# The down product in three stages with some k pairs by seven products

## The chip, the cores and the metric

The kernel runs on one core of a Trainium2 chip. The metric is the device time of one execution in microseconds. TensorE (PE) multiplies, VectorE (DVE) and ScalarE (ACT) work element by element, and the queue of SyncE (SP) starts the loads. Weights stream from the chip's main memory (HBM) into on-chip memory (SBUF); products are accumulated in eight banks (PSUM).

## The reference

One layer of a decoder on 256 tokens of width 2048, in float32. After a recurrent mixer and an attention mixer have been added to the residual stream, a feed-forward network follows, which is what the change touches:

```python
h = rmsnorm(x, g_ffn[i])
gu = h @ w_ffn_gu[i]                 # 2048 -> 2 x 5632
g, u = jnp.split(gu, 2, axis=-1)
x = x + (jax.nn.silu(g) * u) @ w_ffn_down[i]   # 5632 -> 2048
ple_gate = jax.nn.sigmoid(rmsnorm(x, g_ple[i]) @ w_ple_gate[i])
x = x + ple_gate * (p[i] @ w_ple_proj[i])
```

## The kernel before

Everything is cut into tiles of 128. The 256 tokens are two token tiles, the inner dimension of a product is a row of k tiles (44 for the down product), and the output columns are handled 1024 at a time: a *group* is two blocks of 512 columns for both token tiles, so four output blocks, each in one PSUM bank (called "2", "4", "3", "8" in the code).

**A product in three matmuls.** Each float32 operand is split into a high part that PE takes exactly and a low remainder. One 128 x 128 x 512 product is then three matmuls, high by high, high by low and low by high (`prod`, lines 565 to 567). The tokens are the stationary operand, 512 columns of weights move.

**Two ways to do k tiles.** A *plain* k tile gives four products (two token tiles, two column blocks). A *pair* of k tiles can also be done as a 2 x 2 block product by seven products in place of eight (the method of Strassen and Winograd). Its slots carry names: "11", "21" and "22" for plain quadrants of the weights, "T1" to "T4" for sums of quadrants. The weight sums are made on DVE (`summed`, lines 251 to 281), the sums on the token side by `half_sums` (line 569) once per pair. A list of slots says in which order a group works through its sums and plain k tiles; a number in it is a plain k tile. `SEVEN` (line 33) does the pairs 0 and 1 of 16 k tiles by seven products. `SEVEN3` (line 34) does three pairs, where ("S", i, p) are slots of the single pair p. "11", "T2" and "T3" are accumulated in a fifth bank "B", one on top of the other: after each, ACT copies the bank's state into a tile (`group`, line 632), and the differences of these states are later added to or subtracted from the output blocks. In `wo` this adding is done by `fold`, straight into the residual tiles `x1`.

**The stream of weights.** `PLAN` lists every weight tile in the order of use, cut into chunks of up to 1024 columns (one slot of a group is one chunk). `Stream.need` issues loads eight chunks ahead and splits four chunks ahead: ACT makes the high part `whi` (line 296), DVE the low part `wlo` (line 297), each in four buffers. A buffer comes free when PE is done with its chunk. Plain chunks are loaded into the pool `p32`; the quadrants of sum slots go into the pool of tag Q (26 tiles of 1024 columns), which also holds the normed input `hg`, its sums `hsum` and the activations `acts`. The tag H (21 tiles of 512) holds `x1` and the copies of banks.

**The order.** Instructions are emitted in program order; a planner that knows estimated durations sets the order on each engine before the launch and may move independent instructions past each other. `pend` is a list of small pieces of work (transposes of what the last group made) of which each group takes one per slot from its fourth slot on.

**The feed-forward part** is the last third of `TAIL` (lines 172 and 173): eleven gate and up groups of 512 hidden columns each (`gu`, line 1113, three pairs by seven products over 16 k tiles), each giving two pairs of activation k tiles, and between them the down product, which adds to `x1` what the finished activations give. Before, it comes in four stages of 12, 12, 12 and 8 k tiles, two groups each, and all its k tiles are plain (`down`, line 1133): behind gu 3, gu 6, gu 10 and the third stage. The stage dn0 does not need the activations of gu 3, which precedes it. After the last stage, `next_h` (line 1071) turns `x1` into `h3`, the input of the last product, pg.

Of the kernel before, what the change touches and what calls it, by code (L numbers as in the profile page):

```python
# [11 lines left out]
ALU = mybir.AluOpType  # L12

P = 128
S = 256
# [11 lines left out]
NPR = KR // 2  # L27
NPD = KD // 2
NHP = 8
FQ = [12, 12, 12, 8]  # L30
FQ0 = [0, 12, 24, 36]
NG = 11
SEVEN = ["11", "T1", "21", 4, 5, "22", 6, 7, "T2", 8, 9, "T3", 10, 11, "T4", 12, 13, 14, 15]
SEVEN3 = ["11", ("S", 1, 2), "T1", "21", ("S", 2, 2), 6, "T2", 7, "22", 8, ("S", 3, 2), 9, "T3", 10,
          ("S", 4, 2), 11, "T4", 12, 13, 14, 15]
LONG = ["11", "T1", "21", 4, 5, "22", 6, 7, 8, "T2", 9, 10, 11, "T3", 12, 13, 14, "T4", 15, 16, 17, 18, 19, 20, 21]
TWO = (0, 1)
LAST_GROUP = ("pg", 1)
# [3 lines left out]

def pairs_of(name):

    return (0, 1, 2) if name == "gu" else (0, 1)


# [2 lines left out]
    return isinstance(x, str) or isinstance(x, tuple) and x[0] == "S"  # L50


def products(x):


    if isinstance(x, int):
        return [("2", (x, 0), None, 0), ("4", (x, 1), None, 0), ("3", (x, 0), None, 1), ("8", (x, 1), None, 1)]
    bank = {"11": "B", "T1": "8", "T2": "B", "T3": "B", "21": "2", "22": "3", "T4": "4"}
    if isinstance(x, str):
        return [(bank[x], x, p, c) for c, p in enumerate(TWO)]  # L60
    k = {1: ("11", "21"), 2: ("T1", "T2"), 3: ("22", "T3"), 4: ("T4",)}[x[1]]
    return [(bank[y], y, x[2], c) for c, y in enumerate(k)]

# [22 lines left out]
def plan():  # L86

    out = []

    def dense(w, m, ks, tag=0, nt=2):  # L90
        out.append(((w, m, tag), [(w, k, m + e) for k in ks for e in range(nt)]))

    def proj(c0, p):
        dense("in", c0 + 2 * p, range(KD))

    def gates(p):
        t = []
        for w in ("rga", "rgx"):
            for e in range(2):
                t += [(w, k, 2 * p + e) for k in rg_k_tiles(2 * p + e)]  # L100
        if len(t) <= 16:
            out.append((("rg", p), t))
        else:
            h = len(t) // 2
            out.append((("rg", p), t[:h]))
            out.append((("rg2", p), t[h:]))

    def block(c0, b):

        out.append((("blk", c0, b), [("in", k, c0 + 4 * b + e) for k in range(KD) for e in range(4)]))  # L110

    def tokens(name, g, w, cols, slots):


        for x in slots:
            if isinstance(x, int):
                t = [(w, x, m) for c in cols for m in c]
            elif x[0] == "x":
                t = [("pp", k, m) for k in range(2) for m in cols[x[1]]]
            elif isinstance(x, tuple):  # L120
                p = 2 * x[2]
                t = {1: [(p, 0), (p + 1, 0)], 2: [(p + 1, 1), (p, 1)]}.get(x[1], [])
                t = [(w, k, m) for k, c in t for m in cols[c]]
            elif x in ("T2", "T3", "T4"):
                t = []
            else:
                r, c = {"11": (0, 0), "21": (1, 0), "22": (1, 1), "T1": (0, 1)}[x]
                t = [(w, 2 * p + r, m) for p in TWO for m in cols[c]]
            out.append((("tok", name, g, x), t))

    for stage, g, w, c0, c1, slots in HEAD:
        tokens(stage, g, w, [list(range(c, c + 4)) for c in (c0, c1)], slots)
    proj(C_XR, 0)
    proj(C_XR, 1)
    for p in range(NPR):
        proj(C_GR, p)
        if p + 2 < NPR:
            proj(C_XR, p + 2)
        gates(p)
        if p in GATE_R_AT:  # L140
            block(C_GTR, GATE_R_AT[p])

    for stage, g, w, c0, c1, slots in TAIL:
        if w is None:
            block(c0, g)
            continue
        tokens(stage, g, w, [list(range(c, c + 4)) for c in (c0, c1)], slots)
    return out
# [4 lines left out]
def tail():  # L153


    def wide(name, w, slots, c=0):
        return [(name, g, w, c + 8 * g, c + 8 * g + 4, slots[g]) for g in range(2)]

    def blocks(*cs):
        return [("blk", b, None, c, None, None) for c, b in cs]  # L160

    def gu(*gs):
        return [("gu", g, "gu", 4 * g, 44 + 4 * g, SEVEN3) for g in gs]

    def dn(q):
        return wide(f"dn{q}", "dn", [list(range(FQ0[q], FQ0[q] + FQ[q]))] * 2)

    x = [("x", 0), ("x", 1)]
    plain = [list(range(KD))] * 2
    return (wide("ro", "ro", [LONG] * 2) + wide("v", "in", [SEVEN] * 2, C_V)  # L170
            + blocks(*[(c, b) for b in range(4) for c in (C_Q, C_K)], *[(C_GTA, b) for b in range(4)])
            + wide("ao", "ao", plain) + wide("wo", "wo", [SEVEN] * 2) + gu(0, 1, 2, 3) + dn(0) + gu(4, 5, 6) + dn(1)
            + gu(7, 8, 9, 10) + dn(2) + dn(3)
            + wide("pg", "pg", [SEVEN[:-3] + x + SEVEN[-3:]] * 2))


# [166 lines left out]
def tile_hybrid_block(ctx: ExitStack, tc: tile.TileContext, xT: bass.AP, x: bass.AP, pT: bass.AP,  # L343
# [25 lines left out]
    def tt(o, a, b, op):  # L369
        nc.vector.tensor_tensor(o, a, b, op)  # L370
# [48 lines left out]
    for n in ("h", "l"):  # L419
        t = cst.tile([P, 512], F32R, tag=f"w1{n}", name=f"w1{n}")  # L420
# [25 lines left out]
    def parts(t):  # L446
        v = t.rearrange("p (e x s) -> p e x s", e=2, x=2)
        return v[:, :, 0, :], v[:, :, 1, :]
# [4 lines left out]
    def split(src, tag):  # L453
        t = tl(tag, F32R)
        hi, lo = parts(t)
        actv(hi, pair(src), AF.Copy)
        tt(lo, pair(src), f32(hi), ALU.subtract)
        return t
# [152 lines left out]
    xg = []  # L611
# [20 lines left out]
    def group(at, pairs, sums, after=None, also=()):  # L632
# [6 lines left out]
        name, g = at  # L639
        slots = [x for n, y, _, _, _, sl in HEAD + TAIL if (n, y) == at for x in sl  # L640
                 if isinstance(x, int) or is_sum(x)]
        seq = [(n, q) for n, x in enumerate(slots) for q in products(x)]
        if at == LAST_GROUP:
            k = len(slots) - 3
            rest = [q for q in seq if q[0] >= k]
# [210 lines left out]
        tt(c22, q8, c22, ALU.subtract)  # L856
        return c11, c21, c12, c22

    def xg_sums(p):
        h = tl("T")  # L860
        hi, lo = parts(xg[p])
        tt(pair(h), f32(hi), f32(lo), ALU.add)
        xsum[p] = half_sums(h)

    def last_gate():
        with behind_splits():
# [5 lines left out]

    n = len(LONG)
    for g in range(2):
        also = {n - 2 + i: (lambda p: lambda: xg_sums(p))(p) for i, p in enumerate(pairs_of("v"))} if g else {
            8: last_gate, 12: next_table}
        for i, c in enumerate(whole(("ro", g), y, ysum, also)):
            o = gtr[2 * g + i // 2][i % 2]
            tt(o, c, o, ALU.mult)
# [168 lines left out]
    x1 = [[None] * 4 for _ in range(2)]  # L1048
    ssq = [cst.tile([P, 8], F32, tag=f"ssq{i}", name=f"ssq{i}") for i in range(2)]

    def squares(i, t, b):
        q = tl("T")
        actv(q, x1[t][b], AF.Square, accum_out=ssq[i][:, 2 * b + t:2 * b + t + 1])
# [36 lines left out]
    for g in range(2):  # L1090
        for b in (2 * g, 2 * g + 1):
            for t in range(2):
                x1[t][b] = tl("C")
                nc.sync.dma_start(x1[t][b], x[t * P:t * P + P, b * 512:b * 512 + 512])

        def fold(tiles):
            for n, (c, op) in enumerate((("11", ALU.add), ("T3", ALU.add), ("T1", ALU.add),
                                         ("T3", ALU.subtract))):
                o = x1[n % 2][2 * g + n // 2]
                tt(o, o, tiles[c], op)  # L1100

        for n, ps in enumerate(group(("wo", g), mix, msum, fold)[0]):
            t, b = n % 2, 2 * g + n // 2
            tt(x1[t][b], ps, x1[t][b], ALU.add)
            squares(0, t, b)
        for p in range(4 * g, 4 * g + 4):
            pend.append(next_h(hg, hsum, p, PC_GF))
    token_scales(0, rs1)


    acts = {}

    def gu(g):
        c11, c21, c12, c22 = whole(("gu", g), hg, hsum)
        for c, t in ((c11, 0), (c21, 1)):
            actv(c, c, AF.Silu, scale=rs1[:, t:t + 1])
        for c, t, s_ in ((c12, 0, c11), (c22, 1, c21)):
            stt(c, c, rs1[:, t:t + 1], s_, ALU.mult, ALU.mult)

        def turn(f):  # L1120
            def run():
                ps = psum()
                for e in range(2):
                    for t, a in enumerate((c12, c22)):
                        c = (2 * f + e) * P
                        o = e * 256 + t * P
                        nc.tensor.transpose(ps[:, o:o + P], a[:, c:c + P], ident)  # L1127
                acts[2 * g + f] = split(ps, "A" if (2 * g + f) % 11 < 8 else "B")
            return run

        pend.extend(turn(f) for f in range(2))

    def down(q, g):
        for n, ps in enumerate(group((f"dn{q}", g), acts, None)[0]):
            t, b = n % 2, 2 * g + n // 2
            tt(x1[t][b], ps, x1[t][b], ALU.add)
            if q == 3:
                squares(1, t, b)
        if q == 3:
            for p in range(4 * g, 4 * g + 4):  # L1140
                pend.append(next_h(h3, sum3, p, PC_GP))

# [105 lines left out]
```

## Time and profile before

| | |
|---|---|
| median of 3 runs | 1884.11 us (1883.82 to 1884.48) |
| profiled execution, own time | 1884.7 us |
| its span | 1883.0 us |
| mean granted clock of TensorE | 0.998 |
| busy PE, DVE, ACT | 1873.4, 1377.9, 1158.5 us |
| matmuls | 9000 |
| main memory read | 357.69 MB |

A row of the view of groups reads: line, engine, operation, result <- operands (by the program's tile names), partitions x elements, xcount | busy time of the group in us, mean ns of one | idle time of the engine ahead of it and what ended it. Since matmuls are pipelined, the time from start to end of one is longer than its share of PE. In the view by stretches a row is one stretch of time (from:to in us from the span's start), its length, and for each engine its busy time and its count of instructions. A row of the timeline is start, length, engine, line, operation. Most token and weight work goes through helpers, so that line 370 is every `tensor_tensor` of the tiles and line 376 every activation of the main part.

### The profile page before, as it was taken

The page shows a single profiled execution, that of the slowest core. Times are in us where ns is not written, and L with a number is a line of the kernel's source. Part 1 is how long each engine was busy: PE and PEld are TensorE (multiplying, and loading weights), DVE is VectorE, ACT ScalarE, POOL GpSimd, SP SyncE. Part 2 cuts the span into 40 slices and gives each one's busy share as a digit, 9 for nine tenths or more (in the row PEclk, how much of TensorE's full clock was granted, in tenths as well). Part 3 has the DMA queues.
Part 4 walks back from the last instruction along what each step waited for, and adds up shares of the span by engine and source line. Part 5 has one row for each costly group of instructions (what it writes and reads, how often), then busy time and mean ns, then how long its engine had stood idle before and what let it go on. Part 6 is the DMA issues. An engine that isn't in the chain of part 4 may idle for free.

```text
span 1883.0 us, 24009 instructions
## 1 busy us (share of the span) xinstructions
PE 1873.4 (99%) x9000; PEld 1576.0 (84%) x9000; DVE 1377.9 (73%) x1649; ACT 1158.5 (62%) x1535; POOL 2.2 (0%) x9
## 2 busy tenths in 40 slices
PE   9999999999999999999999999999999999999998
PEld 7899989888888888888888888888888888888886
DVE  7688887677776576665578988767886688855776
ACT  6688888764554566776356765644554466543673
POOL 0000000000000000000000000000000000000000
PEclk9999999999999999999999999999999999999999
DMA  7456555665545545445556565375447645465554
GB/s 275 180 181 197 191 178 192 231 210 196 205 156 191 190 158 167 157 157 179 190 216 227 189 239 211 129 262 210 173 145 263 211 151 216 148 214 193 168 192 140
DMA packets 101925, 361.36 MB, mean 192 GB/s; under 512 B 11440, under 2 KB 12080, under 8 KB 101808
## 3 DMA queue, kind: packets, MB, share of 16 engines
q1 hardware_dynamic: 101664, 359.82, 55.4%
q8 instruction: 70, 1.15, 0.2%
q14 instruction: 47, 0.39, 0.1%
q10 hardware_dynamic: 144, 0.01, 0.0%
HBM read 357.69 MB, written 2.10 MB: 191 GB/s over the span
## 4 chain that ended last, share of the span: by engine, by line
PE 99%; DMA 0%; DVE 0%; SPq 0%; ACT 0%; issue 0%; DVEq 0%
PE ps L567 27%; PE ps L566 27%; PE ps L565 27%; PE ps L495 9%; PE ps L499 4%; PE ps L479 1%; PE ps L478 1%; PE ps L477 1%; PE ps L1127 1%; DMA w<-in_w_dram 0%; PE ps L919 0%; PE ps L1068 0%; DVE H L370 0%; PE ps L1030 0%; PE ps L973 0%; PE ps L972 0%
## 5 line engine op out<-in xcount | busy, mean ns | idle before, releaser
L297 DVE TENSOR_TENSOR wlo<-w,whi 128x1024 fp32r<-128x1024 f32 (+1 forms) x580 | 701.1, 1215 | 370.1 <-ACT whi L296 365.2
L296 ACT ACTIVATE whi<-w 128x1024 fp32r<-128x1024 f32 (+1 forms) x580 | 607.4, 1052 | 461.9 <-PE ps L567 402.4
L566 PE MATMUL ps<-wlo,Q 128*128 128x512 f32 x2223 | 866.4, 390 | 0.1
L567 PE MATMUL ps<-whi,Q 128*128 128x512 f32 x2223 | 866.0, 390 | 0.0
L565 PE MATMUL ps<-whi,Q 128*128 128x512 f32 x2223 | 792.5, 392 | 0.0
L566 PEld LDWEIGHTS ps<-wlo,Q 128*128 128x128 f32 x2223 | 417.5, 188 | 86.4 <-DVE wlo L297 1.3
L567 PEld LDWEIGHTS ps<-whi,Q 128*128 128x128 f32 x2223 | 417.4, 188 | 86.6
L565 PEld LDWEIGHTS ps<-whi,Q 128*128 128x128 f32 x2223 | 417.0, 188 | 85.5 <-ACT whi L296 0.8
L296 ACT ACTIVATE whi<-Q 128x1024 fp32r<-128x1024 f32 (+1 forms) x177 | 182.6, 1032 | 132.2 <-PE ps L567 112.3
L297 DVE TENSOR_TENSOR wlo<-Q,whi 128x1024 fp32r<-128x1024 f32 (+1 forms) x177 | 210.1, 1189 | 50.3 <-ACT whi L296 50.1
L495 PE MATMUL ps<-Q,whi 128*128 128x512 f32 x704 | 170.7, 392 | 0.0
L495 PEld LDWEIGHTS ps<-Q,whi 128*128 128x128 f32 x704 | 128.7, 188 | 24.5
L370 DVE TENSOR_TENSOR H<-ps,H 128x512 f32<-128x512 f32 (+1 forms) x166 | 95.9, 607 | 24.8 <-PE ps L567 16.0
L280 DVE TENSOR_TENSOR Q<-Q,Q 128x1024 f32<-128x1024 f32 x76 | 92.8, 1221 | 0.9
L499 PEld LDWEIGHTS ps<-Q,wlo 128*128 128x128 f32 x704 | 90.4, 191 | 3.5
L376 ACT ACTIVATE H<-ps 128x512 f32<-128x512 f32 (+1 forms) x126 | 62.7, 518 | 48.1 <-PE ps L567 30.1
L499 PE MATMUL ps<-Q,wlo 128*128 128x256 f32 x704 | 91.5, 283 | 0.0
L376 ACT ACT_TABLE_LOAD x53 | 68.0, 1283 | 0.9
L370 DVE TENSOR_TENSOR H<-H,H 128x512 f32<-128x512 f32 (+2 forms) x111 | 65.8, 601 | 1.1 <-ACT H L376 0.6
L376 ACT ACTIVATE Q<-H 128x512 fp32r<-128x512 f32 x41 | 25.1, 625 | 26.2 <-DVE H L370 25.5
L479 PE MATMUL ps<-Q,wlo 128*128 128x256 f32 x140 | 39.6, 283 | 0.0
L478 PE MATMUL ps<-Q,whi 128*128 128x256 f32 x140 | 39.6, 283 | 0.0
(132 smaller groups left out, 869.2 us busy)
## 6 DMA issues: line engine op xcount, KB each, us to landing
w<-in_w_dram SPq DMA_DIRECT2D x558, 512.0 KB, 4.0
Q<-in_w_dram SPq DMA_DIRECT2D x98, 512.0 KB, 6.2
w<-in_w_dram SPq DMA_DIRECT2D x16, 448.0 KB, 3.2
H<-in_x_dram SPq DMA_DIRECT2D x8, 256.0 KB, 6.1
H<-in_xT_dram SPq DMA_DIRECT2D x7, 256.0 KB, 6.9
out_dram<-H SPq DMA_DIRECT2D x7, 256.0 KB, 3.2
w<-in_w_dram SPq DMA_DIRECT2D x4, 320.0 KB, 4.3
w<-in_w_dram SPq DMA_DIRECT2D x2, 256.0 KB, 2.8
```

The lines of the kernel that those rows point to most:

```text
L280: self.nc.vector.tensor_tensor(r[o], r[o], r[a], ALU.add)
L296: self.hi_ins = self.nc.scalar.activation(hi[:, :c], t[:, :c], AF.Copy)
L297: self.lo_ins = self.nc.vector.tensor_tensor(lo[:, :c], t[:, :c], hi[:, :c].bitcast(F32), ALU.subtract)
L370: nc.vector.tensor_tensor(o, a, b, op)
L376: nc.scalar.activation(o, i, f, **kw)
L478: nc.tensor.matmul(o, wt[0], xl, start=False, stop=False)
L479: nc.tensor.matmul(o, wt[1], xh, start=False, stop=stop)
L495: nc.tensor.matmul(pss[e], wt[0], rhs(xs, k), start=(k == 0), stop=(k == n - 1))
L499: nc.tensor.matmul(pss[e][:, :256], wt[1], rhs(xs, k)[:, :256], start=False, stop=False)
L565: nc.tensor.matmul(ps, x[0], wh, start=start, stop=False, skip_group_check=goes_on)
L566: nc.tensor.matmul(ps, x[0], wl, start=False, stop=False, skip_group_check=goes_on)
L567: nc.tensor.matmul(ps, x[1], wh, start=False, stop=stop, skip_group_check=goes_on)
```

## The change

The down product is cut into three stages of 16, 16 and 12 k tiles. dn0 comes behind gu 0 to 3, dn1 behind gu 4 to 7, dn2 behind gu 8 to 10, so that each stage uses all the activations made so far, those of the group just before it included. dn0 and dn1 do their first two k pairs by seven products, with the list `SEVEN` shifted to their k tiles; dn2 does its first pair so, with a new list `ONE`. The token-side sums of these pairs are made by `parts_sums` (formerly `xg_sums`, which did the same for `xg`) near the end of the gu group ahead (at slots 17 and 18 of 0 to 20; in gu 10 at slot 17 alone). `fold` becomes `onto_x1` and serves both wo and the down product. All activations take the same tile tag.

```diff
-FQ = [12, 12, 12, 8]
-FQ0 = [0, 12, 24, 36]
+FQ = [16, 16, 12]
+FQ0 = [0, 16, 32]
...
+def ONE(k):
+
+    return [("S", 1), ("S", 2), k + 2, k + 3, k + 4, ("S", 3), k + 5, k + 6, ("S", 4), *range(k + 7, k + 12)]
...
+    if name[:2] == "dn":
+        q = int(name[2])
+        return [FQ0[q] // 2 + i for i in range(2 if FQ[q] == 16 else 1)]
     return (0, 1, 2) if name == "gu" else (0, 1)
...
-def products(x):
+def products(x, two=TWO):
...
-        return [(bank[x], x, p, c) for c, p in enumerate(TWO)]
+        return [(bank[x], x, p, c) for c, p in enumerate(two)]
...
     def dn(q):
-        return wide(f"dn{q}", "dn", [list(range(FQ0[q], FQ0[q] + FQ[q]))] * 2)
+        k, p = FQ0[q], FQ0[q] // 2
+        slots = [x if isinstance(x, str) else x + k for x in SEVEN] if FQ[q] == 16 else [
+            x if isinstance(x, int) else x + (p,) for x in ONE(k)]
+        return wide(f"dn{q}", "dn", [slots] * 2)
...
-            + wide("ao", "ao", plain) + wide("wo", "wo", [SEVEN] * 2) + gu(0, 1, 2, 3) + dn(0) + gu(4, 5, 6) + dn(1)
-            + gu(7, 8, 9, 10) + dn(2) + dn(3)
+            + wide("ao", "ao", plain) + wide("wo", "wo", [SEVEN] * 2) + gu(0, 1, 2, 3) + dn(0) + gu(4, 5, 6, 7) + dn(1)
+            + gu(8, 9, 10) + dn(2)
...
-    def xg_sums(p):
+    def parts_sums(pairs, sums, p):
         h = tl("T")
-        hi, lo = parts(xg[p])
+        hi, lo = parts(pairs[p])
         tt(pair(h), f32(hi), f32(lo), ALU.add)
-        xsum[p] = half_sums(h)
+        sums[p] = half_sums(h)
...
+    def onto_x1(g):
+
+        def run(tiles):
+            for n, (c, op) in enumerate((("11", ALU.add), ("T3", ALU.add), ("T1", ALU.add),
+                                         ("T3", ALU.subtract))):
+                o = x1[n % 2][2 * g + n // 2]
+                tt(o, o, tiles[c], op)
+        return run
...
-    acts = {}
+    acts, asum = {}, {}
+    behind = {3: 0, 7: 1, 10: 2}
 
     def gu(g):
-        c11, c21, c12, c22 = whole(("gu", g), hg, hsum)
+        also = {}
+        if g in behind:
+            also = {17 + i: (lambda p: lambda: parts_sums(acts, asum, p))(p)
+                    for i, p in enumerate(pairs_of(f"dn{behind[g]}"))}
+        c11, c21, c12, c22 = whole(("gu", g), hg, hsum, also)
...
-                acts[2 * g + f] = split(ps, "A" if (2 * g + f) % 11 < 8 else "B")
+                acts[2 * g + f] = split(ps, "A")
...
     def down(q, g):
-        for n, ps in enumerate(group((f"dn{q}", g), acts, None)[0]):
+        for n, ps in enumerate(group((f"dn{q}", g), acts, asum, onto_x1(g))[0]):
             t, b = n % 2, 2 * g + n // 2
             tt(x1[t][b], ps, x1[t][b], ALU.add)
-            if q == 3:
+            if q == 2:
                 squares(1, t, b)
-        if q == 3:
+        if q == 2:
```

More of the change, by code (lines that the diff above doesn't have):

```diff
@@ L127, in tokens @@
                 r, c = {"11": (0, 0), "21": (1, 0), "22": (1, 1), "T1": (0, 1)}[x]
-                t = [(w, 2 * p + r, m) for p in TWO for m in cols[c]]
+                t = [(w, 2 * p + r, m) for p in pairs_of(name)[:2] for m in cols[c]]
             out.append((("tok", name, g, x), t))
@@ L641, in group @@
                  if isinstance(x, int) or is_sum(x)]
-        seq = [(n, q) for n, x in enumerate(slots) for q in products(x)]
+        seq = [(n, q) for n, x in enumerate(slots) for q in products(x, pairs_of(name)[:2])]
         if at == LAST_GROUP:
@@ L874, in tile_hybrid_block @@
     for g in range(2):
-        also = {n - 2 + i: (lambda p: lambda: xg_sums(p))(p) for i, p in enumerate(pairs_of("v"))} if g else {
+        also = {n - 2 + i: (lambda p: lambda: parts_sums(xg, xsum, p))(p) for i, p in enumerate(pairs_of("v"))} if g else {
             8: last_gate, 12: next_table}
@@ L1094, in tile_hybrid_block @@
                 nc.sync.dma_start(x1[t][b], x[t * P:t * P + P, b * 512:b * 512 + 512])
[L1096 to L1102, printed above, removed]
+        for n, ps in enumerate(group(("wo", g), mix, msum, onto_x1(g))[0]):
             t, b = n % 2, 2 * g + n // 2
```

## The prediction

> **What bounds the kernel now.** I read the page first: its span, the busy shares, the slices and the chain that ended last.
>
> ```profile
> span 1883.0 us, 24009 instructions
> ...
> PE 1873.4 (99%) x9000; PEld 1576.0 (84%) x9000; DVE 1377.9 (73%) x1649; ACT 1158.5 (62%) x1535; POOL 2.2 (0%) x9
> ...
> PEclk9999999999999999999999999999999999999999
> ...
> PE 99%; DMA 0%; DVE 0%; SPq 0%; ACT 0%; issue 0%; DVEq 0%
> ...
> L566 PE MATMUL ps<-wlo,Q 128*128 128x512 f32 x2223 | 866.4, 390 | 0.1
> L567 PE MATMUL ps<-whi,Q 128*128 128x512 f32 x2223 | 866.0, 390 | 0.0
> L565 PE MATMUL ps<-whi,Q 128*128 128x512 f32 x2223 | 792.5, 392 | 0.0
> ```
>
> PE is busy in 99% of the span, its granted clock is full in every slice, the chain is PE, and the three lines of `prod` hold most of it, 2223 times each. Their idle time (last column) is 0.1 us in all. The view of the waits of PE alone has one row:
>
> ```profile
> PE ps L607 <- DVE ones_r L417: 1.5, 1, 1.5
> ```
>
> So after its first instruction PE waits for nobody, at no group's boundary either. A matmul removed therefore shortens the run by its pitch, unless a new wait takes its place. The 390 ns of a row are not that pitch, since matmuls overlap. The pitch comes from the view by stretches. I found the groups' boundaries by counting products in program order (2223 is exactly what the plan lists, so no record is missing).
>
> ```profile
> core 0: us, PE busy (x) PEld busy (x) DVE busy (x) ACT busy (x) POOL busy (x), PEclk, DMA share, GB/s
> 507.96:550.12 42.16, 42.16 (x187) 34.92 (x186) 32.82 (x33) 22.73 (x24) 0.00 (x0) 1.00 0.44 150
> 890.61:934.13 43.52, 43.52 (x194) 36.04 (x192) 20.24 (x18) 17.98 (x18) 0.00 (x0) 1.00 0.59 193
> 1023.67:1067.70 44.03, 44.03 (x203) 36.50 (x202) 40.92 (x56) 30.48 (x45) 0.00 (x0) 1.00 0.62 221
> 1195.96:1238.38 42.42, 42.42 (x193) 35.13 (x191) 32.61 (x34) 25.79 (x29) 0.00 (x0) 1.00 0.44 147
> 1272.00:1304.64 32.64, 32.64 (x146) 27.04 (x144) 19.32 (x19) 12.73 (x12) 0.00 (x0) 1.00 0.67 245
> 1304.64:1346.12 41.48, 41.48 (x185) 34.36 (x183) 34.19 (x35) 24.08 (x26) 0.00 (x0) 1.00 0.43 140
> 1732.18:1753.94 21.76, 21.76 (x98) 18.02 (x96) 12.11 (x13) 9.22 (x10) 0.00 (x0) 1.00 0.57 193
> 1753.94:1777.63 23.69, 23.69 (x113) 19.59 (x112) 19.00 (x30) 15.95 (x27) 0.00 (x0) 1.00 0.53 179
> ```
>
> In order these are v group 0, ao group 0, wo group 1, gu group 3, dn0 group 1, gu group 4, dn3 group 0 and dn3 group 1. PE's busy time equals the stretch in each. Two of them hold 16 k tiles and nothing but products: ao, all plain, 192 matmuls in 43.52 us, and v, with the list SEVEN, 186 in 42.16 us. Both give 0.2267 us a matmul; dn0 group 1 gives 32.64 / 144 = 0.2267 as well.
>
> **The products removed.** A plain k tile is 4 products of 3 matmuls, so a pair of k tiles is 24 matmuls; by seven products it is 21. Per pair and group 3 x 0.2267 = 0.68 us go. The new stages have 2, 2 and 1 such pairs in 2 groups each: 10 x 0.68 = 6.80 us, 30 matmuls of the 9000. Measured whole, without any pitch: ao minus v is 43.52 - 42.16 = 1.36 us per two-pair group; four of these and two half ones (0.68) are again 6.80 us. Putting 44 k tiles into three parts instead of four removes no matmul by itself, and the transposes stay as many.
>
> **The work added on DVE and ACT.** The prices, from the view of groups that keeps shapes apart:
>
> ```profile
> L297 DVE TENSOR_TENSOR wlo<-w,whi 128x1024 fp32r<-128x1024 f32 x558 | 679.2, 1223 | 359.7 <-ACT whi L296 355.2 <-PE ps L495 0.3
> ...
> L280 DVE TENSOR_TENSOR Q<-Q,Q 128x1024 f32<-128x1024 f32 x76 | 92.8, 1221 | 0.9
> L370 DVE TENSOR_TENSOR H<-ps,H 128x512 f32<-128x512 f32 x118 | 77.3, 685 | 16.6 <-PE ps L567 16.0
> ...
> L373 DVE SCALAR_TENSOR_TENSOR Q<-ps,prm_sb,Q 128x256 fp32r<-128x256 f32 x22 | 9.8, 479 | 0.6 <-ACT Q L376 0.6
> ...
> L370 DVE TENSOR_TENSOR H<-H,H 128x128 f32<-128x128 f32 x22 | 6.1, 286 | 0.1
> ```
> ```profile
> L296 ACT ACTIVATE whi<-w 128x1024 fp32r<-128x1024 f32 x558 | 588.8, 1059 | 455.3 <-PE ps L567 402.4 <-DMA w<-in_w_dram 17.2 <-DVE wlo L297 11.3
> ...
> L376 ACT ACTIVATE H<-ps 128x512 f32<-128x512 f32 x82 | 48.4, 592 | 30.2 <-PE ps L567 30.1
> L376 ACT ACTIVATE Q<-H 128x512 fp32r<-128x512 f32 x41 | 25.1, 625 | 26.2 <-DVE H L370 25.5 <-DVE H L373 0.3
> ```
>
> A two-pair group has 19 chunks: 19 low parts (1.22) and 4 weight sums (1.22), the T2 subtraction and 4 adds into x1 (5 x 0.69), 4 adds from the banks (2.7): 34.2 us of DVE in 42.16 us of PE (81%). ACT: 19 x 1.06 + 4 copies x 0.59 = 22.5 us. Plain 16-tile work would need 16 x 1.22 + 2.7 = 22.2 of DVE, so 12 us come on, four times. The cover has a precedent: wo group 1 runs the same list with the same adds into x1, plus four `next_h`, with DVE at 40.92 of 44.03 us and PE without a gap. I take 0.
>
> The one-pair group has 14 chunks: 13 x 1.22 + 0.69 low parts, four half-width sums (2.7), and the same 6.1 us of adds: 25.4 us in 47 x 3 x 0.2267 = 31.96 us. Group 1 of dn2 takes over dn3's four `next_h`: 2 pairs with half sums (0.69 + 4 x 0.286 + 0.69 = 2.5 each) and 2 without (2 x 0.48, about 1), in all 7: 32.4 us of 33.9 us (31.96 and 1.93 of transposes, 23.69 - 21.76). That is 95%, the tightest place of the change; the same sums of means give wo group 1 42.7 us, where the row has 40.92 and no gap. The last five chunks are plain with 2.72 us of PE against 1.22 of DVE, so the lead is back before pg. I take 0. If the cover went, DVE would end up to 32.4 - 31.96, 0.5 us late.
>
> `parts_sums` adds five times 2.5 us of DVE and 0.62 of ACT in gu 3, 7 and 10; its inputs are made three groups earlier, so nothing forces it between urgent splits, and `xg_sums` does the same twice ahead of v group 0, which has no gap. Without that freedom two calls need 5 us in the last four plain slots, where PE takes 10.9 us and DVE's own four low parts and a sum 6.1: 11.1, 0.2 late. I take 0. Eight adds from banks (5.5 us of DVE) leave with dn3.
>
> **What is moved.** dn0 now uses the pairs 6 and 7 of gu 3, which are turned in its own fourth and fifth slots and first used in its sixteenth, over 20 us later; likewise dn1 and dn2. The turns come after 18 matmuls (4.1 us) of the new group instead of 36 (8.2 us). That is where gu after gu puts them already (gu 3's stretch has eight transposes in its first slots and no gap), so 0.
>
> **The loads.** Bytes stay. 20 transfers go from the w buffers to the Q pool (98 become 118), on the same SP queue in the same order.
>
> ```profile
> w<-in_w_dram SPq DMA_DIRECT2D x558, 512.0 KB, 4.0
> Q<-in_w_dram SPq DMA_DIRECT2D x98, 512.0 KB, 6.2
> ```
>
> A Q transfer lands 2.2 us later than a w one, and is issued eight chunks ahead. Q has 26 buffers; in dn0 I count 8 of hg, 3 of hsum, 8 activations, 2 sums and 4 weight quads: 25. Gu 10 now stands at 8 + 3 + 8 + 7 = 26 without a gap. I take 0.
>
> **The bank shared in dn2.** In ONE, "T2" accumulates in bank B only six matmuls (1.36 us) after "11" ends there, and ACT must have copied "11" in between. No present list is that tight. The nearest rows are the first copies behind the starts of gu 0 (1067.70) and gu 3 (1195.96):
>
> ```profile
> 1071.70 0.58 ACT L376 ACTIVATE H<-ps 128x512 f32<-128x512 f32 x1
> ```
> ```profile
> 1198.73 0.57 ACT L376 ACTIVATE H<-ps 128x512 f32<-128x512 f32 x1
> ```
>
> They end 4.58 us after the start behind four squares, and 3.34 us behind two SiLUs; T2 is due after 9 matmuls, 2.04 us. Left as they stand, PE would wait 1.30 us in dn2's group 0 (behind SiLUs) and 2.54 in group 1 (behind squares): 3.84 us, with every later product queued behind. The other end is 0, not below: a wait gains nothing. PE's order is not the source's, though: where low parts are late, products of high parts run ahead, as in gu 3:
>
> ```profile
> 1200.04 0.84 PE L565 MATMUL ps<-whi,Q 128*128 128x512 f32 x3
> ```
>
> Nine matmuls (2.04 us) of each of the three plain tiles behind S2 need neither copy and can fill that gap. I take 0. [...]
>
> **Sum.** The profiled execution took 1884.7 us (span 1883.0 and 1.7 around it): 1884.7 - 6.8 = 1877.9. The median of the runs is 0.6 lower, 1884.11: 1877.3, a gain of 0.36%. A change within 0.2% (3.8 us) can't be told from none.
>
> **Rivals.** (a) *The copy of "11" holds PE in dn2*: for it the two rows of copies, against it the filling. 1877.3 + 3.84 = 1881.1 if all of it stands, 1879 if half.
>
> (b) *DVE becomes the bound at the new boundaries*: low parts late behind `parts_sums` and the weight sums. For it dn2 group 1 at 95%; against it wo group 1 at 93% without a gap. 0.5 us there and 0.2 at each of three boundaries: 1878.4; three times that if the means mislead, 1880.6.
>
> (c) *Slower: the Q pool runs out.* If the weight quads of a dn group can be issued only when the previous group's activations die, each of the six dn groups starts with the whole transfer and split open: 6.2 + 1.06 = 7.3 us, 44 us in all, 1877.3 + 44 = 1921. It decides from 10.6 us of stalls on (6.8 + 3.8), 1.8 us a group. For it: 25 of 26 buffers by my count; against it: gu 10 at 26 without a gap, and quads that die by the slot of T4. [...]
>
> **How the numbers follow.** The forecast (no stall above 0.7 us) 0.70, with its own range 1876.6 to 1878.0 (the runs spread by 0.4 us on either side); (a) 0.14, half of it within 0.2%; (b) 0.08, mostly still faster; (c) 0.08, of which 0.06 slower. Faster 0.82, same 0.12, slower 0.06. The range goes from 1876.4 to 1881.3, the end of (a) and (b); what is left out is (c) and a little.
>
> **What would show it.** Each `prod` line x2213 instead of x2223, 8970 matmuls; dn0 and dn1 groups of 42.16 us (plus 0.98 for turns in group 0), dn2 of 31.96 plus 0.98 and plus 1.93; no row of PE's waits beyond the first; DVE near 1449 us busy (1377.9 + 4 x 12 + 2 x 8.1 + 5 x 2.5 - 5.5, where 8.1 is 25.4 less the 17.3 of twelve plain tiles). (a) would show as PE waiting for an ACT copy about 2 us into a dn2 group, (b) for L297 behind gu 3, 7 and 10, (c) as SP waits and late Q landings. Wrong I would be if PE gained idle time of several us anywhere between gu 3 and pg.

## The result and the profile after

The changed kernel takes 1879.71 us (median of 11 runs, 1878.9 to 1882.0) against 1884.23 us (11 runs, 1883.58 to 1886.26): a ratio of 0.9977, interval 0.9968 to 0.9986. The gain is 0.23% where 0.36% was forecast. It lies in the stated range, but 2.4 us short of the forecast, and the runs spread over 3.1 us where those of the kernel before mostly lie within 1.

The page after, in the parts that were shown of before (the lines of `prod` are now 576 to 578, the splits 307 and 308, the sums of half quads 266, of whole quads 291):

```profile
span 1878.0 us, 24098 instructions
...
PE 1866.8 (99%) x8970; PEld 1570.1 (84%) x8970; DVE 1440.0 (77%) x1741; ACT 1187.3 (63%) x1580; POOL 2.2 (0%) x9
...
PE 97%; DVE 1%; DMA 1%; issue 0%; SPq 0%; ACT 0%; DVEq 0%
...
L577 PE MATMUL ps<-wlo,Q 128*128 128x512 f32 x2213 | 863.2, 390 | 1.3 <-DVE wlo L308 1.1
L578 PE MATMUL ps<-whi,Q 128*128 128x512 f32 x2213 | 861.8, 390 | 0.0
...
L576 PE MATMUL ps<-whi,Q 128*128 128x512 f32 x2213 | 765.5, 391 | 0.3 <-ACT whi L307 0.3
```

The 30 matmuls are gone. New are the waits of PE, which the view of its waits lists:

```profile
PE ps L618 <- DVE ones_r L428: 1.5, 1, 1.5
PE ps L577 <- DVE wlo L308: 1.1, 2, 0.6
PE ps L576 <- ACT whi L307: 0.3, 1, 0.3
```

The last of these rows is not part of what follows: it lies at 8.99 us, at the start of the kernel. Where the two waits for low parts (`wlo`) are, the view by stretches says. In order: gu 3, dn0 group 0 and 1, gu 4, dn1 group 1, gu 8, dn2 group 0 and 1.

```profile
1195.48:1237.90 42.42, 42.42 (x192) 35.13 (x191) 38.68 (x48) 26.94 (x31) 0.00 (x0) 1.00 0.51 173
1237.90:1281.04 43.14, 43.14 (x195) 35.66 (x194) 35.34 (x38) 23.46 (x26) 0.00 (x0) 1.00 0.59 208
1281.04:1323.20 42.16, 42.16 (x187) 34.92 (x186) 34.37 (x36) 22.00 (x23) 0.00 (x0) 1.00 0.80 286
1323.20:1365.52 42.32, 41.82 (x184) 34.22 (x183) 34.51 (x35) 24.09 (x26) 0.00 (x0) 1.00 0.37 124
1535.92:1578.08 42.16, 42.16 (x187) 34.92 (x186) 33.87 (x35) 22.02 (x23) 0.00 (x0) 1.00 0.79 287
1578.08:1620.92 42.84, 42.11 (x184) 34.16 (x183) 35.00 (x36) 24.09 (x26) 0.00 (x0) 1.00 0.39 123
1705.76:1738.67 32.91, 32.91 (x150) 27.20 (x149) 26.60 (x32) 18.34 (x23) 0.00 (x0) 1.00 0.60 192
1738.67:1772.49 33.82, 33.82 (x159) 28.08 (x157) 26.74 (x40) 23.48 (x38) 0.00 (x0) 1.00 0.60 216
```

All of dn is as forecast to 0.1 us (43.14, 42.16, 32.91 and 33.82 us against 42.16 + 0.98, 42.16, 31.96 + 0.98 and 31.96 + 1.93; dn1 group 0, not shown, takes 43.14 us too). But gu 4 takes 42.32 and gu 8 42.84 us, where 183 matmuls need 41.48, which is what gu 4 took before: 0.84 + 1.36 = 2.2 us more, each in the first 8 us. Only 1.1 us of it are waits in the view; most of the rest lies in rows that count as busy (41.82 and 42.11 us of PE against 41.48). That is the whole shortfall: 1883.0 - 6.8 + 2.2 = 1878.4 of span, 1878.0 measured. The rest of this text is about these two places.

DVE around the start of gu 4 (timeline: start, length, engine, line, operation, and in brackets the idle time before it):

```profile
1317.60 1.23 DVE L291 TENSOR_TENSOR Q<-Q,Q 128x1024 f32<-128x1024 f32 x1
1319.31 0.69 DVE L266 TENSOR_TENSOR Q<-Q,Q 128x512 f32<-128x512 f32 x1 [0.49 <-DMA Q<-in_w_dram]
1319.92 1.22 DVE L308 TENSOR_TENSOR wlo<-Q,whi 128x1024 fp32r<-128x1024 f32 x1
1321.06 1.22 DVE L291 TENSOR_TENSOR Q<-Q,Q 128x1024 f32<-128x1024 f32 x1
1322.19 0.69 DVE L266 TENSOR_TENSOR Q<-Q,Q 128x512 f32<-128x512 f32 x1
1322.79 0.69 DVE L266 TENSOR_TENSOR Q<-Q 128x512 f32<-128x512 f32 x1
```

Three half sums stand between the low parts, and the first waits 0.49 us for a load (0.99 us ahead of gu 8) while a low part is queued behind it. In gu 8 the wait is longer, and so is the loss.

### The profile page after: what moved, and what is told of

The parts are those of the page before. It is cut to its first block, busy times and chain, and to the rows that moved or that the text cites. A ratio compares the mean times of both kernels' runs of the same rounds, so it can differ in the third digit from the quotient of the medians.

```text
span 1878.0 us, 24098 instructions
## 1 busy us (share of the span) xinstructions
PE 1866.8 (99%) x8970; PEld 1570.1 (84%) x8970; DVE 1440.0 (77%) x1741; ACT 1187.3 (63%) x1580; POOL 2.2 (0%) x9
## 4 chain that ended last, share of the span: by engine, by line
PE 97%; DVE 1%; DMA 1%; issue 0%; SPq 0%; ACT 0%; DVEq 0%
PE ps L577 26%; PE ps L578 26%; PE ps L576 26%; PE ps L506 9%; PE ps L510 4%; PE ps L490 1%; PE ps L489 1%; PE ps L488 1%; DMA Q<-in_w_dram 1%; DVE wlo L308 1%; DVE H L381 1%; PE ps L1146 1%; PE ps L930 0%; PE ps L1088 0%; DMA w<-in_w_dram 0%; DVE Q L291 0%
## 5 line engine op out<-in xcount | busy, mean ns | idle before, releaser
L308 DVE TENSOR_TENSOR wlo<-w,whi 128x1024 fp32r<-128x1024 f32 (+2 forms) x560 | 675.8, 1214 | 289.7 <-ACT whi L307 284.7
L578 PE MATMUL ps<-whi,Q 128*128 128x512 f32 x2213 | 861.8, 390 | 0.0
L307 ACT ACTIVATE whi<-w 128x1024 fp32r<-128x1024 f32 (+2 forms) x560 | 586.0, 1052 | 371.2 <-PE ps L578 324.3
L576 PE MATMUL ps<-whi,Q 128*128 128x512 f32 x2213 | 765.5, 391 | 0.3 <-ACT whi L307 0.3
L307 ACT ACTIVATE whi<-Q 128x1024 fp32r<-128x1024 f32 (+1 forms) x213 | 219.8, 1033 | 182.2 <-PE ps L578 140.3
L308 DVE TENSOR_TENSOR wlo<-Q,whi 128x1024 fp32r<-128x1024 f32 (+1 forms) x213 | 253.1, 1189 | 64.6 <-ACT whi L307 64.5
L291 DVE TENSOR_TENSOR Q<-Q,Q 128x1024 f32<-128x1024 f32 x92 | 112.4, 1221 | 1.6 <-DMA Q<-in_w_dram 0.3
L387 ACT ACTIVATE H<-ps 128x512 f32<-128x512 f32 (+1 forms) x150 | 77.0, 531 | 57.6 <-PE ps L578 39.5
L381 DVE TENSOR_TENSOR H<-ps,H 128x512 f32<-128x512 f32 (+1 forms) x158 | 90.8, 603 | 19.2 <-PE ps L578 10.1
L381 DVE TENSOR_TENSOR H<-H,H 128x512 f32<-128x512 f32 (+2 forms) x151 | 88.7, 597 | 5.8 <-ACT H L387 5.1
```

The costliest lines, as they stand in the source:

```text
L291: self.nc.vector.tensor_tensor(r[o], r[o], r[a], ALU.add)
L307: self.hi_ins = self.nc.scalar.activation(hi[:, :c], t[:, :c], AF.Copy)
L308: self.lo_ins = self.nc.vector.tensor_tensor(lo[:, :c], t[:, :c], hi[:, :c].bitcast(F32), ALU.subtract)
L387: nc.scalar.activation(o, i, f, **kw)
L576: nc.tensor.matmul(ps, x[0], wh, start=start, stop=False, skip_group_check=goes_on)
L578: nc.tensor.matmul(ps, x[1], wh, start=False, stop=stop, skip_group_check=goes_on)
```

## The experiments

Each is compared with the kernel before on the same chip; the time in brackets is that of before. The theories carry the numbers of the expectations.

**The parts alone.** The regrouping without sevens, the two pairs of dn0 and dn1 alone, and the one pair of dn2 alone. The edit, with the set of stages that keep their sevens:

```diff
     def dn(q):
+        if q not in ():        # (0, 1) and (2,) in the other two
+            return wide(f"dn{q}", "dn", [list(range(FQ0[q], FQ0[q] + FQ[q]))] * 2)
         k, p = FQ0[q], FQ0[q] // 2
...
-    behind = {3: 0, 7: 1, 10: 2}
+    behind = {}                # {3: 0, 7: 1} and {10: 2}
```

> The three stages of 16, 16 and 12 k tiles alone, all plain: 9000 matmuls as before. Theory 1: no lists with sums ahead of gu 4 and gu 8 and no new PE wait, 1884.2 us within 0.8. Rival 2 (activations that keep Q buffers to the end of a stage delay the loads of gu 4 and gu 8): PE waits about 2 us there in this kernel too, 1886.

> dn0 and dn1 as changed, dn2 all plain: 24 matmuls fewer than before, 5.44 us. Theory 1: the two waits at gu 4 and gu 8 stay, 1884.2 - 5.4 + 2.0 = 1880.8 us. Rival a of the prediction (what was lost was lost in dn2's shared bank): no loss here, 1878.8.

> dn2 as changed, dn0 and dn1 all plain: 6 matmuls fewer than before, 1.36 us. Theory 1: no wait of PE at gu 4 and gu 8 and none in dn2, 1884.2 - 1.4 = 1882.8 us. Rival a: the loss of 2 us or more shows here, 1884.8 or more.

The regrouping: 1884.69 us (1883.93), ratio 1.0004, 0.9995 to 1.0013. The two pairs: 1881.22, ratio 0.9987, 0.9978 to 0.9995. The one pair: 1883.11, ratio 0.9995, 0.9986 to 1.0004. Against before that is +0.8, -2.7 and -0.8 us, where the matmuls alone give 0, -5.4 and -1.4. In the traces the two pairs have gu 4 at 42.54 and gu 8 at 42.31 us; the other two kernels have both at 41.73 to 41.77. So most of the loss goes with the sevens of dn0 and dn1; the regrouping brings about 0.25 us at each place, and rival (a), a loss in dn2, is out.

**Holding the sums of gu 4 and gu 8.** The first reading was that the half sums at the start of gu 4 are gu 4's own. So every weight sum of these two groups, whole and half, is held behind the low part of the chunk before its slot.

```diff
-                t, c = self.summed(mode)
+                if PLAN[i][0][1:3] in (("gu", 4), ("gu", 8)):
+                    with self.tc.issue_after(self.lo_ins.ins):
+                        t, c = self.summed(mode)
+                else:
+                    t, c = self.summed(mode)
```

> The changed kernel, with the weight sums of gu 4 and gu 8 alone held behind the low part of the chunk before them on DVE, so that no half sum due in the fifth slot can stand ahead of the low parts of the second and third. Theory 1 (DVE order: early half sums, the first of them waiting for its load, make DVE some 2 us late at these two boundaries): PE's waits of 0.8 and 1.3 us there go, the ratio to before falls from 0.9977 to about 0.9965, about 1877.6 us. Rival 2 (the loads come late because Q buffers come free late, whatever the order): PE still waits about 2 us, 1879.7. Rival 3 (the low parts are late because DVE has too much work there): the waits stay or grow, 1879.7 or more.

1882.66 us (1883.93), ratio 0.9993, 0.9985 to 1.0002: 3 us worse than the changed kernel. gu 4 and gu 8 grew by 1.7 and 1.1 us:

```profile
1322.54:1366.52 43.98, 43.02 (x184) 33.96 (x183) 37.38 (x39) 23.78 (x26) 0.00 (x0) 1.00 0.42 150
1579.08:1623.05 43.97, 42.97 (x184) 33.97 (x183) 37.39 (x39) 23.78 (x26) 0.00 (x0) 1.00 0.43 151
```

The miss was read as theory 1 falling, and loads that come too late because the Q pool is full became the next theory (4). For it spoke that before the change the six quads for gu 4 were issued at 1249.5 to 1252.7 us, 52 to 55 us ahead of gu 4, while in the changed kernel five of the six are issued within 35 us of it (1288.0 to 1299.9 us, gu 4 from 1323.2), and those of gu 5 at 1305.0 to 1313.2 us, seven of these eleven when PE's last use of a tile releases a buffer. (What this run really showed came out later, below.)

**The size of the Q pool.** Only the numbers of buffers change: `"Q": (28, 1024), "H": (17, 512)`, then 27 and 19, both at the same memory as 26 and 21, then 25 and 21, one Q buffer fewer.

> The changed kernel with 28 Q buffers in place of 26 (and 17 H buffers in place of 21, the same memory). Theory 4 (Q pool: since dn's own quads and its 8 activations and 2 sums fill the pool, the quads of gu 4 and gu 8 come just ahead of their group, where the kernel before had them some 50 us ahead, so their weight sums fall among the urgent low parts): two more buffers let these loads start earlier, PE's 2 us of waits at gu 4 and gu 8 fall to below 0.7, about 1878.0 us or less, unless 17 H buffers make waits of their own. Theory 3 (too much DVE work at the boundary, whenever the loads come): waits unchanged, 1879.7.

> The changed kernel with 27 Q and 19 H buffers, the list SEVEN as it is. If the count of buffers alone decides, the waits at gu 4 and gu 8 lie below those with 26 (2 us in all), about 1878.8 us. If it is the order that the planner makes of it (28 buffers gave 1.7 and 0.5 us of waits, 25 gave 0.6 and 0.6), any sum between 0.5 and 2.5 us is possible, and only the early list is a remedy.

> The changed kernel with 25 Q buffers in place of 26, H as it is. Theory 4: the loads come later still, PE's waits at gu 4 and gu 8 grow from 2 us to 3 or more, 1881 us or more, perhaps with waits at other boundaries. Theory 3: no change, 1879.7.

28 buffers: 1878.94 us (1884.25), ratio 0.9972, 0.9961 to 0.9982. 27: 1880.53 (1884.09), 0.9980, 0.9971 to 0.9989. 25: 1878.78 (1884.25), 0.9971, 0.9960 to 0.9983. So theory 4's dose is not there: one buffer less did no harm, and gu 4 took 43.25 us with 28 buffers, 42.83 with 27, 42.32 with 26, 42.05 with 25. These are single executions, and the one with 28 was the slowest of its seven (1880.12 us); gu 8 shows no such order (41.97, 42.92, 42.84 and 42.05 us). With 28, the first half sum ahead of gu 4 stood two low parts earlier and waited 3 us for its load:

```profile
1317.02 0.69 DVE L266 TENSOR_TENSOR Q<-Q,Q 128x512 f32<-128x512 f32 x1 [3.01 <-DMA Q<-in_w_dram]
1317.63 1.22 DVE L308 TENSOR_TENSOR wlo<-w,whi 128x1024 fp32r<-128x1024 f32 x1
```

With 25 it stood behind the low parts of the second and third slots:

```profile
1321.57 1.22 DVE L308 TENSOR_TENSOR wlo<-Q,whi 128x1024 fp32r<-128x1024 f32 x1
1322.70 1.88 DVE L381 TENSOR_TENSOR H<-ps,H 128x512 f32<-128x512 f32 x3
1324.50 0.68 DVE L266 TENSOR_TENSOR Q<-Q,Q 128x512 f32<-128x512 f32 x1
```

So the loss goes with the place of the half sums in DVE's order and with the wait for their load, not with the count of buffers. What is left with 25, 0.57 us in gu 4 and in gu 8, was not followed; the waits of PE listed there, 0.5 us in all, are for a copy by ACT.

**A list that frees the buffers earlier.** The same work, T4 in the eleventh slot:

```diff
+SEVEN_E = ["11", "T1", "21", 4, "22", 5, "T2", 6, "T3", 7, "T4", 8, 9, 10, 11, 12, 13, 14, 15]
...
-        slots = [x if isinstance(x, str) else x + k for x in SEVEN] if FQ[q] == 16 else [
+        slots = [x if isinstance(x, str) else x + k for x in SEVEN_E] if FQ[q] == 16 else [
```

> The changed kernel with 26 Q buffers, dn0 and dn1 by a list in which the slots 22, T2, T3 and T4 stand earlier (T4 in the 11th place in place of the 15th), so that the two pairs, their sums and the quads of a dn group come free some 10 us earlier. The work is the same. Theory 4: the quads of gu 4 and gu 8 start earlier, PE's waits there fall below 1 us, about 1878.3. Theory 3: waits unchanged, 1879.7, or new ones inside dn0 and dn1, where the sums now stand closer.

> The early list with 27 Q buffers and 19 H buffers. Theory 4: no PE wait of note at gu 4 and gu 8, 1877.6 us. Theory 3: as the early list with 26.

1878.09 us (1884.25), ratio 0.9966, 0.9954 to 0.9979, and with 27 buffers 1877.78, 0.9965, 0.9953 to 0.9978. With 26, the three half sums stand where the changed kernel has them, but their loads have landed, so DVE no longer waits; gu 4 and gu 8 take 41.75 and 41.78 us. With 27, they are done before the last low parts of dn0, and both take 41.48:

```profile
1312.51 1.42 DVE L267 TENSOR_TENSOR Q<-Q,Q 128x512 f32<-128x512 f32 x2 [1.25 <-PE ps L579]
1313.85 0.68 DVE L267 TENSOR_TENSOR Q<-Q 128x512 f32<-128x512 f32 x1
1314.45 2.35 DVE L309 TENSOR_TENSOR wlo<-w,whi 128x1024 fp32r<-128x1024 f32 x2
```

**Leaving out the half sums of gu 4 and gu 8.** The slots take a quad as it was loaded, so the output of these two groups is not the reference's.

```diff
             _, i, p = mode
+            if skip:
+                t = r["S", 1 if i in (1, 4) else 2, p]
+                return (t[:, 512:], 512) if i == 4 else (t, 1024)
...
-                t, c = self.summed(mode)
+                t, c = self.summed(mode, PLAN[i][0][1:3] in (("gu", 4), ("gu", 8)))
```

> The changed kernel, with the four half-width weight sums of the third pair left out in gu 4 and in gu 8 (their slots take a loaded quad as it is, so the output of these two groups is not the reference's). Loads, chunks and matmuls stay. Theory 5 (PE's 2 us of waits come from DVE being late there, because these sums, made tens of us ahead before, now fall among the low parts, the first of them behind a load): without them DVE is not late, PE's waits at gu 4 and gu 8 go, about 1877.7 us. If the late loads alone hold PE (theory 2), the waits stay, 1879.7.

1881.67 us (1884.09), ratio 0.9986, 0.9977 to 0.9995: slower than with the sums, gu 4 at 42.75 and gu 8 at 44.28 us. This miss solved it, since three half sums still stood at the start of gu 4, the first with a wait of 1.04 us for its load (2.56 us ahead of gu 8). The planned order of the changed kernel on DVE, with buffer numbers, tells whose they are (chunk 519 is the second slot of gu 4; the numbers 688 and 691 are quads of gu 5, 694 its sum):

```
wlo_518 <- Q_671, whi_518
Q_671 <- Q_671, Q_673
Q_694 <- Q_688, Q_691      (half sum, gu 5)
wlo_519 <- Q_672, whi_519
Q_673 <- Q_673, Q_677
Q_694 <- Q_694, Q_691      (half sum, gu 5)
Q_691 <- Q_691             (half sum, gu 5)
```

They belong to gu 5 and are due some 50 us later: the low part of the slot that uses the first two is made at 1370.15 us. The trace agrees: its rows come in this order, and the load that ends the wait, landed at 1319.23 us, is the 67th of the 118 Q loads, of which 56 come ahead of gu 4 and six belong to each gu group. gu 4's own half sums, all but the one due last, are made in dn0 group 1, between the low parts of chunks 512 and 513. So holding gu 4's own (the run above) moved good work into the bad place, where ACT waited 1.7 us for one of them, and gu 5's then stood behind the low parts of chunks 523 and 524. With gu 4's left out, the planner put all three of gu 5's before the low part of chunk 519.

**Holding the half sums of gu 5 and gu 9** behind the low part of k tile 7 of gu 4 and gu 8:

```diff
+                if PLAN[i][0][1:3] in self.held and isinstance(mode, tuple):
+                    with self.tc.issue_after(self.held[PLAN[i][0][1:3]].ins):
+                        t, c = self.summed(mode)
+                else:
+                    t, c = self.summed(mode)
...
+            if PLAN[i][0] in (("tok", "gu", 4, 7), ("tok", "gu", 8, 7)):
+                self.held["gu", PLAN[i][0][2] + 1] = self.lo_ins
```

> The changed kernel, with the half-width weight sums of gu 5 and gu 9 held on DVE behind the low part of the slot of plain k tile 7 in gu 4 and gu 8. Nothing else is moved by hand, the pools are as they are. Theory 6 (the three half sums that stand between the low parts at the starts of gu 4 and gu 8 are not those groups' own but those of gu 5 and gu 9, due some 45 us later; the planner put them there because their loads come in time for it, and on the chip the first waits for its load with the low parts queued behind): PE's waits of 0.8 and 1.4 us go to below 0.3 in all, ratio about 0.9965, 1877.7 us, with runs closer together. If the half sums are not the cause, 1879.7 as with the changed kernel.

> The same hold with the early list of dn0 and dn1, 26 Q buffers. Theory 6: no wait left to remove beyond the hold alone, 1877.6 us, the 30 matmuls in full. If what remained with the early list (0.3 us at each of the two boundaries) was something else, it stays, 1878.1.

1877.63 us (1884.05), ratio 0.9965, 0.9952 to 0.9977, runs from 1877.14 to 1877.79; with the early list 1877.26, ratio 0.9964, 0.9950 to 0.9978. The stretches of gu 4 and gu 8 with the hold alone, and all that PE waits for:

```profile
1322.70:1364.18 41.48, 41.48 (x185) 34.35 (x183) 34.19 (x35) 24.08 (x26) 0.00 (x0) 1.00 0.42 127
1576.88:1618.36 41.48, 41.48 (x185) 34.35 (x183) 34.19 (x35) 24.07 (x26) 0.00 (x0) 1.00 0.41 127
```
```profile
PE ps L625 <- DVE ones_r L435: 1.5, 1, 1.5
```

Both waits are gone with six half sums moved and nothing else edited. The gain is 6.4 us, with the early list 6.8 us, which is what 30 matmuls are worth. With the early list, the hold takes gu 4 and gu 8 from 41.75 and 41.78 us to 41.48: the half sums cost 0.27 and 0.30 us at this place even where they wait for no load. Both kernels beat the changed one as well as the one before (no run of theirs, on another chip, is as long as its shortest, 1878.9 us), and with either the five runs lie within 0.8 us of each other: the spread of the changed kernel went with these waits too.

## Why the prediction came out as it did

*The products removed* was right: 30 matmuls, 0.68 us per pair and group. The dn stretches agree to 0.1 us, and the kernels without the two waits gain 6.4 to 6.8 us.

*The bank shared in dn2*, taken at 0, was right, for the reason given. In group 0, ACT has copied "11" at 1708.17 us, 0.4 us after T2 was due (1705.76 + 2.04), and PE is meanwhile on products of the next plain tile (three matmuls of line 576 in a row):

```profile
1707.59 0.58 ACT L387 ACTIVATE H<-ps 128x512 f32<-128x512 f32 x1
```
```profile
1707.80 0.84 PE L576 MATMUL ps<-whi,Q 128*128 128x512 f32 x3
```

*The work added on DVE and ACT* was right in amount (DVE 1440 us against 1449), in dn2 group 1, the place called tightest (26.74 of 33.82 us busy, less than the 32.4 forecast, since 12 low parts fall in it where 14 were counted, and none of the half sums), and behind gu 3, 7 and 10, where no wait arose.

*The loads* is the step that failed, with "I take 0" and "issued eight chunks ahead". Sum quads were never bound to eight chunks: the planner issued those of gu 4 some 50 us ahead in the kernel before. Two things changed, and the kernels with the parts alone tell them apart. The first is the place of gu 5's half sums. Before, they stood behind the eighth and ninth low parts of gu 4 (1314.88 to 1317.22 us). With the regrouping alone, which has no quads of dn, they stand as in the changed kernel behind the first and second, ahead of gu 4 (from 1325.92 us), but wait for nothing:

```profile
1321.45 0.69 DVE L268 TENSOR_TENSOR Q<-Q,Q 128x512 f32<-128x512 f32 x1
1322.06 1.22 DVE L310 TENSOR_TENSOR wlo<-Q,whi 128x1024 fp32r<-128x1024 f32 x1
1323.19 1.22 DVE L293 TENSOR_TENSOR Q<-Q,Q 128x1024 f32<-128x1024 f32 x1
1324.33 0.69 DVE L268 TENSOR_TENSOR Q<-Q,Q 128x512 f32<-128x512 f32 x1
1324.93 0.69 DVE L268 TENSOR_TENSOR Q<-Q 128x512 f32<-128x512 f32 x1
```

This goes with a loss of 0.25 us at each place, close to the 0.27 and 0.30 us of the early list. The second is the load: with the sevens of dn0 and dn1, which take quads of the same pool, the last quad that the first half sum needs lands only at 1319.23 us, when DVE is already waiting for it, and the loss grows to 0.84 and 1.36 us. DVE has little time to give there: it is busy 34.51 of the 42.32 us of gu 4, against 19.32 of 32.64 us in a plain group before. Rival (b) had the right engine but three other boundaries, rival (c) the right kind of load but a wrong mechanism: no load of an urgent quad held PE, but an early sum that waited for its load, with urgent low parts behind it. PE's waits in gu 4 and gu 8 of the changed kernel are for low parts (0.50 and 0.62 us), none for a load, and DVE's for the load are 0.49 and 0.99 us. The loss at the two places, taken at 0, measured 2.2 us.

That 1879.71 us lies in the range is in part luck. The forecast's own case, no stall above 0.7 us, did not come, and the room above it was made for rivals (a) and (b), at whose places nothing was lost.

In DVE's order nothing ran ahead of the half sum that waited: the high part of chunk 519 was done at 1319.02 us, and its low part started at 1319.92, behind that sum (its row is shown above). The row of the high part:

```profile
1317.96 1.06 ACT L307 ACTIVATE whi<-Q 128x1024 fp32r<-128x1024 f32 x1 [1.66 <-DMA w<-in_w_dram]
```

Two things stay open. Why the planner puts gu 5's half sums ahead of gu 4 once the stages are regrouped is not shown. That they are also the cause of the 0.25 us with the regrouping alone is argued from their place; no run holds them in that kernel.

## What to carry to other kernels

Here PE was busy in 99% of the span, and once the two new waits were gone, the 30 removed matmuls counted in full (6.8 us of 6.80 with the hold and the early list). The prediction fell short by the places where helper work lands in other engines' queues. Look for them also one stage behind the change: here a planner put work that was not yet due ahead of urgent work, and the load of that work landed late (DVE waited 0.49 and 0.99 us for it, and 2.2 us were lost). Before pinning an instruction, find out by its operands whose it is; two runs here moved or left out the wrong one and made things worse (1882.66 and 1881.67 us against 1879.71).

## What was not expected of the hardware

The same wait of a half sum for its load is in the kernel before, and five times as long as in gu 4 after:

```profile
1260.69 0.69 DVE L255 TENSOR_TENSOR Q<-Q,Q 128x512 f32<-128x512 f32 x1 [2.49 <-DMA Q<-in_w_dram]
```

It cost nothing there (PE's only wait in that kernel is the 1.5 us at its start). It fell in a plain group: the low part queued behind it, the eleventh of twelve, was done at 1262.52 us, about 4 us ahead of its slot (an estimate from the group's end at 1272.00 us less two k tiles of 2.72 us). The six quads issued at 1249.5 to 1252.7 us in that kernel landed one after another, after 4.7, 6.8, 7.6, 8.4, 9.1 and 10.5 us, where the next five, issued one at a time from 1277.6 to 1299.4 us, took 3.6 to 4.5. The median of 6.2 us that the prediction used hides this, and the sum waited until 1260.69 us for the fifth of the six, which landed at 1260.59.
